# Opening of a hybrid decoder block: two quarters of x turned one unit sooner, two groups of sums moved with them

## The chip, the cores and the metric

The kernel runs on one core of a Trainium2 chip. The core has a matrix engine (TensorE, PE in the profile), three engines for elementwise work (VectorE or DVE, ScalarE or ACT, GpSimd or POOL), and SyncE (SP), which here issues nearly all loads. Each engine works through its own instructions in the order in which the program issues them; semaphores tie the engines together. The metric is the device time of one execution in microseconds (us); a kernel's time is the median of its runs.

## The reference

For one sequence of 256 rows and width 2048 the reference computes one decoder layer and a last normalisation, all in float32:

```
x = x + 0.5 * swiglu_ffn(rms_norm(x, ffn1_norm), gate, up, down)      # width 5632
z = rms_norm(x, mix_norm) @ w_in                                      # two head groups share z
y = concat(rms_norm(recurrent(z), ...), rms_norm(short_conv(z), ...))
x = x + y @ w_out
x = x + 0.5 * swiglu_ffn(rms_norm(x, ffn2_norm), gate, up, down)
out = rms_norm(x, final_norm)
swiglu_ffn(x, g, u, d) = (silu(x @ g) * (x @ u)) @ d
```

The change lies in the first some 50 us of the first feed-forward part: the first 512 columns of `x @ gate` and `x @ up`.

## The kernel before, in words

Every float32 matrix is multiplied in two parts. ACT copies it into a high part (`hi`, type fp32r), DVE subtracts that from the original and gives the low part (`lo`). A product is high by high, high by low and low by high, three matmuls of 128 x 128 by 128 x 512 each. For the stationary side x has to lie with its columns on the partitions, so x is turned: PE transposes 128 x 128 blocks into a PSUM bank, ACT scales the result by the norm's gain and writes the high part, DVE the low part. This is called a turn of a quarter of x (512 of the 2048 columns; tile `xT_n`). Eight transposes, four ACT copies and four DVE operations make one turn; `turn(c)` in `begin` (line 866) makes PE's part at once and returns two functions, `his` (ACT) and `los` (DVE).

The opening (`begin`, line 845) handles the first 512 columns of gate and up in eight units: quarter 0 to 3 of x with the gate block ("g") and with the up block ("u"). Its names: `fetch(u, m)` loads a unit's weights, `high` and `low` make its two parts on ACT and DVE, `mm` makes its 24 matmuls (16 with the high part of the weights, then 8 with the low part). `multiply` (line 436) has places at which a function can be called within a unit: `late` before the last eighth's low matmuls of the second half of the rows, `within` before the last four high matmuls when the unit is cut into pieces `js`. The order of instructions in `begin` is that of the text of the program, on every engine: nothing is rearranged.

Three weight rooms are used in turn, so a load waits on SP until the low part of the unit three loads earlier has been made; loads behind it on SP wait too.

After the opening the columns of gate and up are computed by a scheme with seven products instead of eight, of sums of quarters and sums of weights. The sums of x that it needs are made within the opening: `sums` (line 794) makes the first one, its high part on ACT and its low part on DVE (tile `xs`), and leaves five further steps to `more_sums(n)`: "two" (two additions), the parts of sum 5, the parts of sum 6, "last" (one addition), and the parts of sum 2. They need quarters 0 and 1 only. `fifth_sums` (line 812) makes the same for one block of 128 columns of quarters 2 and 3: six small DVE additions, a copy on ACT and a low part on DVE. `plain` makes the exact values of a quarter, `norm.squares` the sums of squares on ACT, and `norm.factor` the row factor, which needs all four quarters' squares (a few tiny DVE operations around a square root on ACT).

The order of the stage behind the opening (`fine_stage`, line 1406) is written by a planner that takes the engines' state at the end of the opening as constants (line 1583: `free = {"PE": 0.0, "DVE": -6.0, "ACT": -8.0, "SP": -14.0}`), so its order is the same before and after this change. Its first product ("p0") uses `raw_g_w` with `xT_n` into `ps_g_a`, its second ("p4") uses a sum of two weight blocks with `xs` into `ps_g_c`; then come the transposes `ph`, and a part with `raw_g_x` into `ps_g_e`. Between the low part of p0 and that of p4, DVE adds the weight blocks and multiplies the gated result of the opening (tile `sg`).

Of the kernel before, what the change touches and what calls it, by code (L numbers as in the profile page):

```python
# [176 lines left out]
def hybrid_block(ctx: ExitStack, tc: tile.TileContext, a: dict, out: bass.AP):  # L177
# [43 lines left out]
    def f32(ap):  # L221
        return ap.bitcast(F32)
# [82 lines left out]
    def big(name):  # L305

        return bigs.tile([P, UK, 2 * S], F32R, tag="big", name=name)
# [106 lines left out]
    def low_part(raw, hi, lo):  # L414
        dve.tensor_tensor(lo, raw, f32(hi), op=ALU.subtract)


    def blocks(hi, lo):
        return [(hi[:, j, :], lo[:, j, :]) for j in range(hi.shape[1])]
# [12 lines left out]
    def stationary(tile, t):  # L432

        return [(tile[:, j, t * P : (t + 1) * P], tile[:, j, S + t * P : S + (t + 1) * P]) for j in range(UK)]
# [212 lines left out]
    def quad(tile):  # L647
        return tile.rearrange("p (j c) -> p j c", j=UK)
# [107 lines left out]
    def ffn(tag, norm, after, opening=False):  # L756
        with tc.tile_pool(name=f"ffn{tag}", bufs=1, side="left", reuse_waits="tile") as fp:
            wg, wu, wd = (a[f"ffn{tag}_w_{s}"][0] for s in ("gate", "up", "down"))

            def keep(name, dt=F32):  # L760
                return fp.tile([P, CW], dt, tag="keep", name=name, bufs=11)
# [23 lines left out]
            def quads():  # L785
                if norm.exact is None:
                    return vs
                return {
                    (t, i): norm.exact[:, :, i * S + t * P : i * S + (t + 1) * P] for t in range(NT) for i in range(2)
                }  # L790
# [3 lines left out]
            def sums(meanwhile=None):  # L794
                pair = [big(f"xs{tag}_{i}") for i in range(2)]
                parts = [(b[:, :, o : o + P], b[:, :, o + P : o + S]) for b in pair for o in (0, S)]
                spare = quad(keep(f"spare{tag}"))
                two, last, high, low = seven_of(sf, units[halves[0]], units[halves[1]], quads(), spare, parts, meanwhile)

                def both(i):  # L800
                    high(i)
                    low(i)

                sum_of.extend([two, lambda: both(5), lambda: both(6), last, lambda: both(2)])

            def more_sums(n):
                for _ in range(n):
                    sum_of.pop(0)()
# [3 lines left out]
            def fifth_sums():  # L812
                v, w = keep(f"fifth{tag}"), keep(f"fifth_sums{tag}")
                for i, u in enumerate(plains):
                    x = f32(units[u])[:, 0]
                    dve.tensor_tensor(v[:, i * S : (i + 1) * S], x[:, :S], x[:, S:], op=ALU.add)
                (a11, a21), (a12, a22) = ([v[:, i * S + t * P : i * S + (t + 1) * P] for t in range(NT)] for i in range(2))
                s4, s5, s6, s2 = (w[:, i * P : (i + 1) * P] for i in range(4))
                dve.tensor_tensor(s4, a21, a22, op=ALU.subtract)
                dve.tensor_tensor(s6, a11, a21, op=ALU.subtract)  # L820
                dve.tensor_tensor(s5, s4, a11, op=ALU.subtract)
                dve.tensor_tensor(s2, a12, s5, op=ALU.add)
                home = units[halves[0]]
                high, low = (home[:, :, o + P : o + 2 * P] for o in (0, S))
                act.copy(high, quad(w))
                dve.tensor_tensor(low, quad(w), f32(high), op=ALU.subtract)
                fifth.update({i: (high[:, z, :], low[:, z, :]) for z, i in enumerate((4, 5, 6, 2))})
                one, two = ([stationary(units[u], t)[0] for t in range(NT)] for u in plains)
                fifth.update({0: one[0], 1: two[0], 3: two[1]})
# [8 lines left out]
            def first(u, m):  # L838
                return f"{m}{tag}_0_{u}", {"g": wg, "u": wu}[m][u * UK * P : (u + 1) * UK * P, :CW]
# [5 lines left out]
            def begin():  # L845

                raw, parts = {}, {}
                ends = ((0, 2), (2, UK))

                def fetch(u, m, pieces=((0, UK),), loaded=None):  # L850
                    n, src = first(u, m)
                    raw[u, m] = load(src, n, pieces, loaded)
                    parts[u, m] = split_tiles(n)

                def high(u, m, pieces=ends):
                    for i, e in pieces:
                        act.copy(parts[u, m][0][:, i:e, :], raw[u, m][:, i:e, :])

                def low(u, m, pieces=((0, UK),)):
                    for i, e in pieces:  # L860
                        low_part(*(z[:, i:e, :] for z in [raw[u, m]] + parts[u, m]))

                def mm(u, m, *more):
                    joint(u, m, blocks(*parts[u, m]), *more)

                def turn(c):
                    norm.xT[c] = big(f"xT_{norm.name}_{c}")
                    return norm.turn_in_steps(c, [xres[:, t, c * CW : (c + 1) * CW] for t in range(NT)], norm.xT[c])

                def products(j, which=slice(0, 2)):  # L870
                    hi, lo = blocks(*parts[0, "g"])[j]
                    for w, n in ((hi, 2), (lo, 1))[which]:
                        for t in range(NT):
                            for i, y in enumerate(stationary(norm.xT[0], t)[j][:n]):
                                pe.matmul(ps["g", t], y, w, start=(j, i) == (0, 0) and w is hi, stop=False, skip_group_check=True)

                quarters = tuple((j, j + 1) for j in range(UK))
                fetch(0, "g", quarters, lambda i: load_x(0, 2 * P) if i == 1 else None)
                for j in range(UK):
                    if j == 2:  # L880
                        products(1, slice(0, 1))
                    norm.turn((j,), True)
                    high(0, "g", quarters[j : j + 1])
                    low(0, "g", quarters[j : j + 1])
                    if j == 1:
                        keep_busy(1)
                        products(0)
                products(1, slice(1, 2))
                for j in range(2, UK):
                    products(j)  # L890

                fetch(0, "u", ends)
                load_x(1)
                fetch(1, "g", ends)
                load_x(2)
                load_x(3)
                js = (range(2), range(2, UK))
                high(0, "u", ends[:1])
                norm.squares(0, (0,))
                low(0, "u", ends[:1])  # L900
                high(0, "u", ends[1:])
                norm.squares(0, (1,))
                low(0, "u", ends[1:])
                plain(0)

                def second():
                    his, los = turn(1)
                    his()
                    los()

                norm.squares(1)
                mm(0, "u", None, None, js, second)

                high(1, "g")
                low(1, "g", ends)
                plain(1)
                norm.squares(2)
                mm(1, "g", None, None, js)

                fetch(1, "u")  # L920
                fetch(2, "g")
                norm.squares(3, (0,))
                high(1, "u", ends[:1])
                norm.squares(3, (1,))
                norm.factor()
                high(1, "u", ends[1:])
                low(1, "u", ends)
                high(2, "g")

                def third():  # L930
                    low(2, "g", ends[:1])
                    his, los = turn(2)
                    his()
                    los()

                mm(1, "u", None, third, js)
                low(2, "g", ends[1:])

                fetch(2, "u")
                high(2, "u")  # L940
                low(2, "u")
                fetch(3, "g")
                high(3, "g")
                sums()
                mm(2, "g")

                his, los = turn(3)
                his()
                los()
                low(3, "g")  # L950
                fetch(3, "u")
                high(3, "u")
                more_sums(1)
                low(3, "u")
                mm(2, "u")
                more_sums(4)
                fifth_sums()
                mm(3, "g")
                mm(3, "u")

# [1022 lines left out]
    with tc.tile_pool(name="outs", bufs=1, side="left", reuse_waits="tile") as op:  # L1983
# [10 lines left out]
        two, last_sum, high, low = seven_of(so, yT[0], yT[1], quads, spare, halves_of)  # L1994
# [148 lines left out]
    ends = {}  # L2143
# [56 lines left out]
```

## Time and profile before

| | |
|---|---|
| median of 3 runs | 1708.05 us (1707.28 to 1708.12) |
| profiled execution, its own time | 1707.82 us |
| its span, first to last instruction | 1706.0 us |
| PE busy | 1694.0 us (99%) |
| DVE busy | 1540.4 us (90%) |
| ACT busy | 1109.0 us (65%) |
| granted TensorE clock, mean | 0.999 |

PE is TensorE's matmuls, PEld its weight loads, which overlap the matmuls; an "q" behind an engine's name means its queue, where loads are issued. A row of the timeline has start, length, engine, line, operation, output and inputs, shapes, count, and in brackets how long the engine stood idle before and what ended the wait. Line 43 is a helper through which all instructions go, so tiles tell the groups apart. A group's length is that from its first start to its last end; instructions of one engine overlap a little at their ends. In a row of the view by stretches, the numbers are the stretch, its length, then for PE, PEld, DVE, ACT and POOL the busy time with the count, the granted clock, the share of the DMA engines and GB/s. A row of waits tells who waited for what, and total, times and longest in us.

### The profile page before, as it was taken

The page shows a single profiled execution, that of the slowest core. Times are in us where ns is not written, and L with a number is a line of the kernel's source. Part 1 is how long each engine was busy: PE and PEld are TensorE (multiplying, and loading weights), DVE is VectorE, ACT ScalarE, POOL GpSimd, SP SyncE. Part 2 cuts the span into 40 slices and gives each one's busy share as a digit, 9 for nine tenths or more (in the row PEclk, how much of TensorE's full clock was granted, in tenths as well). Part 3 has the DMA queues.
Part 4 walks back from the last instruction along what each step waited for, and adds up shares of the span by engine and source line. Part 5 has one row for each costly group of instructions (what it writes and reads, how often), then busy time and mean ns, then how long its engine had stood idle before and what let it go on. Part 6 is the DMA issues. An engine that isn't in the chain of part 4 may idle for free.

```text
span 1706.0 us, 20409 instructions
## 1 busy us (share of the span) xinstructions
PE 1694.0 (99%) x7869; PEld 1411.8 (83%) x7869; DVE 1540.4 (90%) x1330; ACT 1109.0 (65%) x1334; POOL 63.6 (4%) x96
## 2 busy tenths in 40 slices
PE   9999999999999999999999999999999999999998
PEld 7788888888888888888888888888888888888886
DVE  7999899999899999887897887998899998999997
ACT  6675566766666668567966665755666665667665
POOL 0200000000000000000000000000000000000000
PEclk9999999999999999999999999999999999999999
DMA  8777887768877868755565656767768878868784
GB/s 291 216 246 198 275 260 227 236 210 256 250 253 228 286 178 270 243 163 191 175 198 198 216 196 213 255 242 212 244 191 265 271 223 239 284 215 249 246 250 144
DMA packets 184432, 392.51 MB, mean 230 GB/s; under 512 B 7956, under 2 KB 10896, under 8 KB 178832
## 3 DMA queue, kind: packets, MB, share of 16 engines
q1 hardware_dynamic: 174912, 340.81, 57.5%
q0 software_dynamic: 9248, 49.36, 14.9%
q8 instruction: 61, 1.00, 0.2%
q10 hardware_dynamic: 176, 1.06, 0.1%
q14 instruction: 35, 0.29, 0.0%
HBM read 339.82 MB, written 2.10 MB: 200 GB/s over the span
## 4 chain that ended last, share of the span: by engine, by line
PE 98%; DVE 1%; issue 0%; ACT 0%; DVEq 0%
PE ps_in L43 10%; PE ps_u_a L43 10%; PE ps_g_a L43 10%; PE ps_d_a L43 9%; PE ps_u_c L43 6%; PE ps_g_c L43 5%; PE ps_d_c L43 5%; PE ps_u_d L43 4%; PE ps_g_d L43 4%; PE ps_d_d L43 4%; PE ps_d_e L43 4%; PE ps_d L43 4%; PE ps_g_e L43 3%; PE ps_o L43 3%; PE ps_u_e L43 2%; PE ps_g L43 2%
## 5 line engine op out<-in xcount | busy, mean ns | idle before, releaser
L43 ACT CAST hi_g_p<-raw_g_w 128x1024 fp32r<-128x1024 f32 (+1 forms) x140 | 172.6, 1263 | 116.2 <-DVE raw_g_w L43 43.6
L43 ACT CAST hi_u_p<-raw_u_w 128x1024 fp32r<-128x1024 f32 (+1 forms) x140 | 172.7, 1262 | 100.2 <-PE ps_u_a L43 41.6
L43 DVE TENSOR_TENSOR lo_g_p<-raw_g_w,hi_g_p 128x2560 fp32r<-128x2560 f32 (+2 forms) x90 | 199.3, 2227 | 31.9 <-ACT hi_g_p L43 11.5
L43 DVE TENSOR_TENSOR lo_u_p<-raw_u_w,hi_u_p 128x2560 fp32r<-128x2560 f32 (+2 forms) x90 | 199.5, 2228 | 14.4 <-ACT hi_u_p L43 11.6
L43 ACT CAST hi_d_p<-raw_d_w 128x1024 fp32r<-128x1024 f32 x140 | 141.2, 1047 | 79.8 <-DVE raw_d_w L43 39.6
L43 DVE TENSOR_TENSOR lo_d_p<-raw_d_w,hi_d_p 128x2048 fp32r<-128x2048 f32 (+1 forms) x90 | 162.4, 1813 | 11.7 <-ACT hi_d_p L43 10.3
L43 PE MATMUL ps_in<-xT_nm,hi_in 128*128 128x512 f32 x512 | 122.5, 391 | 0.0
L43 PEld LDWEIGHTS ps_in<-xT_nm,hi_in 128*128 128x128 f32 x512 | 94.0, 188 | 18.9 <-ACT tha L43 0.5
L43 ACT CAST hi_d_x<-raw_d_x 128x1024 fp32r<-128x1024 f32 x72 | 73.2, 1047 | 37.1 <-PE ps_d_c L43 11.9
L43 DVE TENSOR_TENSOR lo_in<-raw_in,hi_in 128x2048 fp32r<-128x2048 f32 x32 | 73.3, 2289 | 21.0 <-ACT hi_in L43 20.5
L43 DVE TENSOR_TENSOR lo_d_x<-raw_d_x,hi_d_x 128x2048 fp32r<-128x2048 f32 x36 | 82.1, 2286 | 7.1 <-ACT hi_d_x L43 7.1
L43 DVE TENSOR_TENSOR raw_u_w<-raw_u_w,raw_u_w 128x1024 f32<-128x1024 f32 (+2 forms) x50 | 86.7, 1755 | 0.7
L43 DVE TENSOR_TENSOR raw_g_w<-raw_g_w,raw_g_w 128x1024 f32<-128x1024 f32 (+2 forms) x50 | 86.4, 1754 | 0.8 <-DMA raw_g_w<-in_ffn_w_gate_dram 0.3
L43 ACT CAST hi_in<-raw_in 128x1024 fp32r<-128x1024 f32 x64 | 64.2, 1044 | 30.1 <-PE ps_in L43 16.3
L43 ACT CAST hi_g_x<-raw_g_x 128x1536 fp32r<-128x1536 f32 x40 | 59.2, 1480 | 19.4 <-DMA raw_g_x<-in_ffn_w_gate_dram 11.5
L43 DVE TENSOR_TENSOR lo_u_x<-raw_u_x,hi_u_x 128x1536 fp32r<-128x1536 f32 x40 | 70.1, 1751 | 0.3 <-issue 0.3
L43 DVE TENSOR_TENSOR lo_g_x<-raw_g_x,hi_g_x 128x1536 fp32r<-128x1536 f32 x40 | 70.0, 1751 | 0.0
L43 PEld LDWEIGHTS ps_in<-xT_nm,lo_in 128*128 128x128 f32 x512 | 65.6, 191 | 2.5
L43 ACT CAST hi_u_x<-raw_u_x 128x1536 fp32r<-128x1536 f32 x40 | 59.1, 1476 | 11.5 <-PE ps_u_c L43 5.7
L43 PE MATMUL ps_in<-xT_nm,lo_in 128*128 128x256 f32 x512 | 66.4, 283 | 0.0
L43 PE MATMUL ps_u_a<-hi_u_p,xT_n 128*128 128x512 f32 x240 | 61.1, 390 | 0.0
L43 PE MATMUL ps_g_a<-hi_g_p,xT_n 128*128 128x512 f32 x240 | 60.9, 389 | 0.0
(473 smaller groups left out, 3922.9 us busy)
## 6 DMA issues: line engine op xcount, KB each, us to landing
raw_g_w<-in_ffn_w_gate_dram SPq DMA_DIRECT2D x40, 1024.0 KB, 6.9
raw_u_w<-in_ffn_w_up_dram SPq DMA_DIRECT2D x40, 1024.0 KB, 6.0
raw_d_w<-in_ffn_w_down_dram SPq DMA_DIRECT2D x40, 1024.0 KB, 6.2
raw_d_x<-in_ffn_w_down_dram SPq DMA_DIRECT2D x36, 1024.0 KB, 6.2
raw_in<-in_w_in_dram SPq DMA_DIRECT2D x32, 1024.0 KB, 5.1
raw_g_x<-in_ffn_w_gate_dram SPq DMA_DIRECT2D x40, 768.0 KB, 7.7
raw_u_x<-in_ffn_w_up_dram SPq DMA_DIRECT2D x40, 768.0 KB, 7.1
raw_d_w<-raw_d_w POOLq DMA_DIRECT2D x20, 1024.0 KB, 7.4
```

What stands on the lines that cost most here:

```text
L43: ins = getattr(self.engine, name)(*args, **kwargs)
```

## The change

The third quarter of x is turned inside unit (1, g), before its last four high matmuls, where it was turned inside (1, u) before its last four low ones. The fourth quarter is turned inside (1, u) where it was turned behind (2, g). `sums` is called behind the low part of (1, u), before the parts of (2, g), where it was behind the parts of (2, u) and the high part of (3, g). Its further steps follow between the parts of the later units, and `fifth_sums` stands before the low part of (3, u), where it was behind everything. The low part of (2, g) is no longer split around a turn.

```diff
                 norm.squares(2)
-                mm(1, "g", None, None, js)
+
+                def turning(c):
+                    def fn():
+                        his, los = turn(c)
+                        his()
+                        los()
+
+                    return fn
+
+                mm(1, "g", None, None, js, turning(2))
 
                 fetch(1, "u")
                 fetch(2, "g")
...
                 low(1, "u", ends)
+                sums()
                 high(2, "g")
-
-                def third():
-                    low(2, "g", ends[:1])
-                    his, los = turn(2)
-                    his()
-                    los()
-
-                mm(1, "u", None, third, js)
-                low(2, "g", ends[1:])
+                low(2, "g", ends)
+                mm(1, "u", None, None, js, turning(3))
 
                 fetch(2, "u")
                 high(2, "u")
+                more_sums(1)
                 low(2, "u")
                 fetch(3, "g")
                 high(3, "g")
-                sums()
                 mm(2, "g")
 
-                his, los = turn(3)
-                his()
-                los()
+                more_sums(2)
                 low(3, "g")
+                more_sums(2)
                 fetch(3, "u")
                 high(3, "u")
-                more_sums(1)
+                fifth_sums()
                 low(3, "u")
                 mm(2, "u")
-                more_sums(4)
-                fifth_sums()
                 mm(3, "g")
                 mm(3, "u")
```

## The prediction

> **What bounds the kernel now.** First the page's head, then who waited for whom on TensorE over the whole span, then the same for its weight loads early on, then busy times by stretch.
>
> ```profile
> span 1706.0 us, 20409 instructions
> PE 1694.0 (99%) x7869; PEld 1411.8 (83%) x7869; DVE 1540.4 (90%) x1330; ACT 1109.0 (65%) x1334; POOL 63.6 (4%) x96
> ```
> ```profile
> PE ps_g_c L43 <- ACT hi_g_p L43: 1.8, 2, 1.0
> ...
> PE ps_g_c L43 <- DVE lo_g_p L43: 0.5, 1, 0.5
> ```
> ```profile
> PEld ps_g_e L43 <- DVE lo_g_x L43: 0.3, 1, 0.3
> ```
> ```profile
> 53.47:63.80 10.33, 7.96 (x32) 5.27 (x31) 10.29 (x8) 6.52 (x7) 4.39 (x6) 1.00 0.41 95
> 63.80:98.20 34.40, 34.40 (x156) 28.39 (x155) 33.91 (x21) 23.92 (x24) 5.22 (x11) 1.00 0.77 248
> ```
>
> PE is the bound: in the whole run it waits for data, apart from its very first instruction, only at ps_g_c. That is the second product right behind the opening. In the stretch 53.47 to 63.80 PE is busy 7.96 of 10.33 us while DVE is busy 10.29: there, and there alone, DVE sets the pace. From 63.80 on PE has no gap though DVE works 33.91 of 34.40, so what PE gains before 63.80 it keeps, if DVE gains as much. Now PE in order of time (start, length, count).
>
> ```profile
> 12.50 2.92 PE L43 MATMUL ps_u<-hi_u,xT_n 128*128 128x512 f32 x12
> 15.25 1.04 PE L43 MATMUL pt_n<-ident,xres 128*128 128x128 f32 x8
> ...
> 18.86 3.79 PE L43 MATMUL ps_g<-hi_g,xT_n 128*128 128x512 f32 x16
> ...
> 24.30 3.79 PE L43 MATMUL ps_u<-hi_u,xT_n 128*128 128x512 f32 x16
> ...
> 53.47 2.43 PE L43 MATMUL ps_g_a<-hi_g_p,xT_n 128*128 128x512 f32 x10
> 55.95 1.43 PE L43 MATMUL ps_g_a<-lo_g_p,xT_n 128*128 128x512 f32 x5
> 58.34 1.19 PE L43 MATMUL ps_g_c<-hi_g_p,xs 128*128 128x512 f32 x4 [0.97 <-ACT hi_g_p L43]
> 60.38 1.19 PE L43 MATMUL ps_g_c<-hi_g_p,xs 128*128 128x512 f32 x4 [0.85 <-ACT hi_g_p L43]
> ...
> 63.00 0.73 PE L43 MATMUL ps_g_c<-lo_g_p,xs 128*128 128x512 f32 x2 [0.50 <-DVE lo_g_p L43]
> ...
> 63.80 1.04 PE L43 MATMUL ph<-ident,sg 128*128 128x128 f32 x8
> ```
>
> A unit of 24 matmuls without a turn takes 24.30 - 18.86 = 5.44 us, 0.2267 each. A unit with a turn inside takes 18.86 - 12.50 = 6.36. The 30 matmuls of the first two products (53.47 to 63.80) would take 6.80; they take 10.33, so 3.53 us are lost there. That is what the change can win, with a few tenths of small losses beside it.
>
> **Why DVE is late: it idled before.** ACT first, then DVE.
>
> ```profile
> 15.89 1.57 ACT L43 ACTIVATE xT_n<-pt_n,cols_first 128x256 fp32r<-128x256 f32 x4 [0.98 <-PE pt_n L43]
> 17.33 2.01 ACT L43 CAST hi_g<-raw_g 128x1024 fp32r<-128x1024 f32 x2
> ...
> 20.75 0.64 ACT L43 ACTIVATE junk_n<-xres 128x512 f32<-128x512 f32 x1
> ...
> 21.38 1.03 ACT L43 CAST hi_u<-raw_u 128x1024 fp32r<-128x1024 f32 x1
> ...
> 23.58 1.03 ACT L43 CAST hi_u<-raw_u 128x1024 fp32r<-128x1024 f32 x1
> 24.51 1.99 ACT L43 CAST hi_g<-raw_g 128x1024 fp32r<-128x1024 f32 x2
> 29.48 1.57 ACT L43 ACTIVATE xT_n<-pt_n,cols_first 128x256 fp32r<-128x256 f32 x4 [2.97 <-PE pt_n L43]
> 30.92 2.01 ACT L43 CAST hi_u<-raw_u 128x1024 fp32r<-128x1024 f32 x2
> ...
> 50.62 2.42 ACT L43 CAST hi_g_p<-raw_g_w 128x1024 fp32r<-128x1024 f32 x2
> ...
> 60.23 1.47 ACT L43 CAST hi_g_x<-raw_g_x 128x1536 fp32r<-128x1536 f32 x1
> ```
> ```profile
> 24.37 2.36 DVE L43 TENSOR_TENSOR lo_u<-raw_u,hi_u 128x1024 fp32r<-128x1024 f32 x2
> ...
> 30.35 1.66 DVE L43 SCALAR_TENSOR_TENSOR xT_n<-pt_n,cols_first,xT_n 128x256 fp32r<-128x256 f32 x4 [2.49 <-ACT xT_n L43]
> ...
> 36.63 0.69 DVE L43 TENSOR_TENSOR xs<-spare,xs 128x512 fp32r<-128x512 f32 x1 [0.69 <-ACT xs L43]
> 37.75 1.66 DVE L43 SCALAR_TENSOR_TENSOR xT_n<-pt_n,cols_first,xT_n 128x256 fp32r<-128x256 f32 x4 [0.43 <-ACT xT_n L43]
> ...
> 47.64 0.69 DVE L43 TENSOR_TENSOR xs<-v,xs 128x512 fp32r<-128x512 f32 x1 [0.69 <-ACT xs L43]
> ...
> 50.74 0.69 DVE L43 TENSOR_TENSOR xT_n<-fifth_sums,xT_n 128x512 fp32r<-128x512 f32 x1 [0.69 <-ACT xT_n L43]
> 53.07 2.83 DVE L43 TENSOR_TENSOR lo_g_p<-raw_g_w,hi_g_p 128x2560 fp32r<-128x2560 f32 x1 [1.63 <-ACT hi_g_p L43]
> ...
> 65.67 1.75 DVE L43 TENSOR_TENSOR lo_g_x<-raw_g_x,hi_g_x 128x1536 fp32r<-128x1536 f32 x1
> ```
>
> From the low part of (1, u) at 24.37 to the first product's low part at 53.07 are 28.70 us, of which 2.49 + 0.69 + 0.43 + 0.69 + 0.69 + 1.63 = 6.62 idle: 22.08 of work. The 2.49 is the third quarter's turn (it waits for PE at 29 us), the 1.63 stands behind ACT, which could not begin hi_g_p at 50.62 before the fifth-slice copy.
>
> **The change, part by part.** No instruction is added or removed; eight transposes, four ACT and four DVE operations per turn, three sums groups and their copies change place. The order of loads stays.
>
> *Third quarter's turn inside (1, g).* PE reaches it at 18.86 + (15.25 - 12.50) = 21.61. ACT begins the copies 15.89 - 15.25 = 0.64 later, at 22.25, and is free 17.33 - 15.89 = 1.44 after that, at 23.69. Queued behind these copies on ACT are the fourth quarter's squares, both halves of hi_u of unit 1 and the norm's square root, so all move from 20.75 to 23.69, by 2.94. The fourth quarter's load is not late: its squares ran at 20.75 without a wait. The halves of hi_u end at 21.38 + 1.03 + 2.94 = 25.35 and 23.58 + 1.03 + 2.94 = 27.55. The low part of (1, u) follows the norm's factor on DVE and starts at 24.37 + 2.94 = 27.31.
>
> *PE's new waits.* (1, g) now takes 6.36 and ends at 25.22. (1, u) finds its first half at 25.35 + 0.05 (58.34 against the copy's end), 0.18 late; eight matmuls (1.81) later, at 27.21, it wants the second half, there at 27.60: 0.39. How much a restart costs no row gives alone: sixteen in step take 3.79, so four would take 1.07, and behind a wait they take 1.19, about 0.1. Bounds 0 and 0.2 each; I take 0.1 twice. Together 0.77. The fourth quarter's turn sits inside (1, u): 6.36 again. (1, u) ends at 25.22 + 6.36 + 0.77 = 32.35.
>
> *DVE from 27.31.* The third quarter's 1.66 now lie ahead of this point (in idle time before the factor), so 22.08 - 1.66 = 20.42 of work are left. Of the idle, three waits of 0.69 remain (a sum, its copy on ACT, its low part); the waits for turns and the 1.63 go; one is new: hi_g of unit 2 now stands behind the first sum's copy. That sum is ready at 27.31 + 2.3 + 0.68 = 30.29, its copy ends at 30.9, the half of hi_g (1.99 for two) at 31.9, and DVE, free at 31.66, waits 0.27. So the first product's low part starts at 27.31 + 20.42 + 2.34 = 50.1 instead of 53.07, 3.0 sooner. The sums cost nothing extra: they were on DVE before, and low (3, u), now last, ends at 50.1 where PE wants it 3.6 into that unit, about 52.3. ACT is through with the fifth-slice copy at 47 and with hi_g_p (2.42) at 49.5, before 50.1. If that cover of 0.6 went, its excess would come off the 3.0.
>
> *PE to the end of the stall.* PE wants hi_g of unit 2's second half at 33.26; it ends at 32.9: cover 0.3. Four units of 5.44 lead to 54.11, 0.64 later than now. Then 6.80 for the first two products without a wait, since DVE and the copies between are 3.0 sooner: 60.91 instead of 63.80, a gain of 2.89. The last low part of the second product, due at 60.23, comes 3.0 before 63.00, at 60.0: 0.2 to spare. The next tight place is lo_g_x, which already holds PE's weights for 0.3; on DVE it ends 3.0 sooner, so PE cannot gain more than about 3.0 in any case without DVE gaining more. Sum: 2.9 us.
>
> *Loads.* A load goes out when the low part that frees its room is done.
>
> ```profile
> 26.75 0.37 SPq L43 DMA_DIRECT2D raw_g<-in_ffn_w_gate_dram  x1
> ...
> 45.17 0.92 SPq L43 DMA_DIRECT2D raw_g_w<-in_ffn_w_gate_dram  x2
> 46.13 1.42 SPq L43 DMA_DIRECT2D raw_g_x<-in_ffn_w_gate_dram  x2
> ```
> ```profile
> raw_g<-in_ffn_w_gate_dram SPq DMA_DIRECT2D x1, 1024.0 KB, 5.3
> ```
> ```profile
> DMA to landing us min/median/max: 4.3/5.7/8.5
> ```
>
> The gate columns of unit 3 leave at 29.7 instead of 26.75 and land 5.3 later at 35.0; ACT comes to them about 36. Low (3, u) was done at 45.14 and ends at 50.1 now, so the fourth load of the next stage leaves at 50.2, raw_g_x behind it at 51.1 instead of 46.13. With at most 8.5 to landing it is there by 59.6, by the median 56.8. Its copy (1.47) ran at 60.23 and would now be free to run at 57.3; PE wants it at 60.91 + 0.79 = 61.7. So up to 59.6 + 1.5 = 61.1 it is covered, by 0.6.
>
> The page TensorE: Matmul & The Clock Gate of the Trainium skill (section Architectural detail) says that ACT and DVE are strict first-in first-out. It speaks against the change, as copies that wait for PE now hold the squares and hi_u. The trace agrees: hi_u at 30.92 ran only behind the copies that ACT had waited 2.97 us for. Were ACT free to pass them, the 0.77 would go and the sum be 3.7; by the rule it is 2.9.
>
> **Own time and median.** The profiled execution took 1707.82 us, span 1706.0 and 1.8 around it: 1704.9 after. The median of the runs is 1708.05, so the forecast is 1705.1. I take 0.2% (3.4 us) as what can be told from no change.
>
> **Rivals.**
> - *The whole loss goes.* If (1, u) finds hi_u in time (0.57 of waiting and 0.2 of restarts were overpriced) and DVE's waits shrink likewise, PE gains 3.53 plus the 0.3 at lo_g_x and some tenths: up to 4.2, so 1703.9. For it: half a microsecond decides. Against it: ACT's order is fixed, and the copies cannot start before PE's transposes.
> - *DVE starts later than I count.* Every 1 us by which low (1, u) starts after 27.31, or by which a copy behind ACT holds DVE, comes off the gain. With 2 us: 1707.1. For it: three links (transposes, copies, squares and factor) in a row, with PE waiting too. Against it: each link has its row.
> - *The load takes the stall's place, slower than before.* raw_g_x leaves 5.0 later and its user is 2.9 earlier. If it lands after 64.59 - 1.5 = 63.1 (64.59 is 63.80 + 0.79), 12 us after its issue, nothing is won; at 14 us PE loses 2: 1710. It decides from 61.7 - 1.5 = 60.2 on, 9.1 us after issue. Against it: the longest landing of this kind is 8.5, and the queue is only 0.41 full in 53.47 to 63.80.
> - *It does nothing.* If the stall were due to its own loads or to PE, 1708.0. Against it: the waits at 58.34 to 63.00 name ACT and DVE, and DVE is busy 10.29 of 10.33.
>
> **Chances.** The forecast 0.52, by itself 1704.4 to 1705.9; the whole loss 0.20; DVE late 0.18; the load 0.06; nothing 0.04. The range 1703.7 to 1707.6 leaves out the load, the far end of nothing and the edges, under 0.2. Faster by over 0.2% means under 1704.6: most of the second case and a slice of the first, 0.26. Slower by over 0.2% is the far part of the load, with what I have not thought of, 0.06. The rest, 0.68, is within 0.2%.
>
> **What would show it.** Copies of xT_n on ACT near 22.3 and squares at 23.7; PE waiting at ps_u of unit 1 for hi_u, twice, 0.2 and 0.4; lo_g_p at 50.1 on DVE with no idle ahead of it; PE through ps_g_c without a wait and ph at 60.9; raw_g_x issued near 51. I am wrong if PE still waits at ps_g_c, if raw_g_x appears as a releaser of ACT for more than 3 us, or if low (1, u) starts after 28.

## The result, and the profile after

The changed kernel takes 1704.88 us (median of 20 runs, 1704.42 to 1706.92), the kernel before 1707.74 (20 runs beside it, 1707.28 to 1708.32): 2.86 us less, a ratio of 0.9984 with a 95% interval of 0.9977 to 0.9990. The forecast was 1705.1, a gain of 2.9 us on the 1708.05 of the first three runs. The profiled execution took 1704.92 us with a span of 1703.0.

Who waited for whom on PE over the whole span of the changed kernel (total, times, longest in us):

```profile
span 1703.0 us, 20410 instructions
```
```profile
PE idle L43 <- DVE ones L43: 1.1, 1, 1.1
PE ps_in_c_a L43 <- DVE lo_in_c_p L43: 0.3, 1, 0.3
```

The waits at ps_g_c are gone. A wait of 0.3 us has appeared at ps_in_c_a, at 731.8 us; it is told of below. The stretch in which PE had been busy 7.96 of 10.33 us now reads (stretch, length, busy PE, PEld, DVE, ACT, POOL with counts, clock, DMA share, GB/s):

```profile
53.47:63.80 10.33, 10.33 (x51) 8.67 (x50) 10.33 (x9) 7.09 (x9) 7.35 (x10) 1.00 1.07 324
```

DVE is as full as before, but PE is full as well: DVE's work now lies 3 us ahead. PE in order of time, the rows that answer to those before:

```profile
12.66 2.91 PE L43 MATMUL ps_u<-hi_u,xT_n 128*128 128x512 f32 x12
...
19.02 2.88 PE L43 MATMUL ps_g<-hi_g,xT_n 128*128 128x512 f32 x12
21.74 1.03 PE L43 MATMUL pt_n<-ident,xres 128*128 128x128 f32 x8
...
23.54 1.99 PE L43 MATMUL ps_g<-lo_g,xT_n 128*128 128x512 f32 x8
25.55 3.38 PE L43 MATMUL ps_u<-hi_u,xT_n 128*128 128x512 f32 x12
...
32.39 3.79 PE L43 MATMUL ps_g<-hi_g,xT_n 128*128 128x512 f32 x16
...
54.15 2.43 PE L43 MATMUL ps_g_a<-hi_g_p,xT_n 128*128 128x512 f32 x10
56.41 1.30 PE L43 MATMUL ps_g_a<-lo_g_p,xT_n 128*128 128x512 f32 x5
57.55 1.98 PE L43 MATMUL ps_g_c<-hi_g_p,xs 128*128 128x512 f32 x8
...
60.95 1.03 PE L43 MATMUL ph<-ident,sg 128*128 128x128 f32 x8
```

The first unit here starts at 12.66 instead of 12.50, before anything that was changed, so 0.16 is to be taken from the times of the changed kernel when the two are compared. The price is seen at 25.55: (1, u) starts 0.2 late, and its twelve matmuls last 3.38 where those at 19.02 last 2.88, 0.5 for the second half of hi_u. (The 0.2 is 25.55 against 19.02 + 6.36 = 25.38, the time of a unit with a turn inside.) The gain is seen at 57.55: eight matmuls in one piece, where before they came in two fours with a wait each. From the first unit to ph are 60.95 - 12.66 = 48.29 us; before they were 63.80 - 12.50 = 51.30. That is 3.01 us.

ACT and DVE around the same places:

```profile
22.38 1.57 ACT L43 ACTIVATE xT_n<-pt_n,cols_first 128x256 fp32r<-128x256 f32 x4 [1.51 <-PE pt_n L43]
23.82 0.65 ACT L43 ACTIVATE junk_n<-xres 128x512 f32<-128x512 f32 x1
...
46.65 0.62 ACT L43 CAST xT_n<-fifth_sums 128x512 fp32r<-128x512 f32 x1 [0.59 <-DVE fifth_sums L43]
47.18 2.42 ACT L43 CAST hi_g_p<-raw_g_w 128x1024 fp32r<-128x1024 f32 x2
...
58.38 1.48 ACT L43 CAST hi_g_x<-raw_g_x 128x1536 fp32r<-128x1536 f32 x1 [1.00 <-DMA raw_g_x<-in_ffn_w_gate_dram]
```
```profile
27.45 2.35 DVE L43 TENSOR_TENSOR lo_u<-raw_u,hi_u 128x1024 fp32r<-128x1024 f32 x2
...
32.04 2.36 DVE L43 TENSOR_TENSOR lo_g<-raw_g,hi_g 128x1024 fp32r<-128x1024 f32 x2 [0.26 <-ACT hi_g L43]
...
47.91 2.29 DVE L43 TENSOR_TENSOR lo_u<-raw_u,hi_u 128x2048 fp32r<-128x2048 f32 x1
50.12 2.82 DVE L43 TENSOR_TENSOR lo_g_p<-raw_g_w,hi_g_p 128x2560 fp32r<-128x2560 f32 x1
```

hi_g_p on ACT begins at 47.18 instead of 50.62, and lo_g_p on DVE follows low (3, u) with no idle time at 50.12 instead of 53.07.

The 3 us stay. By plain difference of the times, the group ps_u_a<-hi_u_p, at 131.36 before, has a gain of 2.95 us, and ps_in at 704.33 and 708.07 still 2.95; around 760 it is 2.71, after the new wait at ps_in_c_a, and 2.91 in the last products. So PE carried the gain through without a stall that gave it back; the wait of 0.3 took a part of it for a while, and the last products have it again.

### The profile page after: what moved, and what is told of

It reads as the page before. It is cut to its first block, busy times and chain, and to the rows that moved or that the text cites. A ratio compares the mean times of both kernels' runs of the same rounds, so it can differ in the third digit from the quotient of the medians.

```text
span 1703.0 us, 20410 instructions
## 1 busy us (share of the span) xinstructions
PE 1693.2 (99%) x7869; PEld 1413.0 (83%) x7869; DVE 1540.2 (90%) x1330; ACT 1108.4 (65%) x1334; POOL 63.7 (4%) x96
## 4 chain that ended last, share of the span: by engine, by line
PE 57%; DVE 0%; issue 0%; DVEq 0%; ACT 0%
PE ps_in L43 9%; PE ps_u_a L43 5%; PE ps_g_a L43 5%; PE ps_d_a L43 5%; PE ps_u_c L43 3%; PE ps_g_c L43 3%; PE ps_o L43 3%; PE ps_d_c L43 3%; PE ps_u_d L43 2%; PE ps_g_d L43 2%; PE ps_d_d L43 2%; PE ps_d_e L43 2%; PE ps_d L43 2%; PE ps_g_e L43 2%; PE ps_u L43 1%; PE ps_o_q_x L43 1%
```

## The experiments

Each kernel was timed in five rounds beside the kernel before. The intervals of the ratios are about 0.0009 wide to either side, 1.5 us, so the times alone do not tell apart what differs by less; for that the text goes by the traces, one profiled execution of each kernel. For each run the table gives the stretch from the first matmul of (0, u) to ph, which leaves the start out.

| kernel | median, us (before beside it) | ratio, interval | (0, u) to ph, us | less than before |
|---|---|---|---|---|
| before | | | 51.30 | |
| the change | 1704.88 (1707.74) | 0.9984, 0.9977 to 0.9990 | 48.29 | 3.01 |
| turns only | 1707.00 (1707.82) | 0.9996, 0.9987 to 1.0005 | 50.05 | 1.25 |
| sums only | 1704.71 (1707.82) | 0.9982, 0.9973 to 0.9991 | 48.54 | 2.76 |
| fifth-slice sums last | 1707.81 (1707.82) | 1.0002, 0.9993 to 1.0011 | 51.19 | 0.11 |
| unit (1, u) first | 1703.97 (1707.82) | 0.9977, 0.9968 to 0.9986 | 47.63 | 3.67 |
| before, one line moved | 1706.86 (1707.89) | 0.9993, 0.9984 to 1.0002 | 50.32 | 0.98 |
| the change, work added | 1706.24 (1707.89) | 0.9988, 0.9979 to 0.9997 | 49.45 | 1.85 |
| unit (1, u) first, work added | 1704.10 (1707.89) | 0.9977, 0.9967 to 0.9988 | 47.59 | 3.71 |

**The turns alone.** Against the kernel before:

```diff
-                mm(1, "g", None, None, js)
+                mm(1, "g", None, None, js, turning(2))
...
-                mm(1, "u", None, third, js)
-                low(2, "g", ends[1:])
+                low(2, "g", ends)
+                mm(1, "u", None, None, js, turning(3))
...
                 mm(2, "g")
-
-                his, los = turn(3)
-                his()
-                los()
```

> The kernel before with the two turns moved and nothing else; sums and fifth-slice sums stay behind the units. Theory (DVE's idle time and the copy of the fifth-slice sums ahead of hi_g_p set the stall): the turns give back DVE's 2.49 us of waiting for PE, but start (1, u) 2.9 us later, and hi_g_p on ACT still stands behind the fifth-slice copy, so lo_g_p starts near 52.0 instead of 53.07 (50.1 with the whole change): 1.1 to 1.4 us faster than before, PE still waiting at ps_g_c for about 1.5. Rival (the sooner turns are what wins): 2.5 to 3 us faster, lo_g_p near 50.

Measured 0.8 us less by the medians, under the 1.1 expected and with an interval that holds no change, and 1.25 by the trace, as expected. PE's waits over the span are there again, halved:

```profile
PE ps_g_c L43 <- ACT hi_g_p L43: 0.7, 1, 0.7
PE ps_g_c L43 <- DVE lo_g_p L43: 0.5, 1, 0.5
```
```profile
49.49 0.69 DVE L43 TENSOR_TENSOR xT_n<-fifth_sums,xT_n 128x512 fp32r<-128x512 f32 x1 [0.69 <-ACT xT_n L43]
51.81 2.83 DVE L43 TENSOR_TENSOR lo_g_p<-raw_g_w,hi_g_p 128x2560 fp32r<-128x2560 f32 x1 [1.63 <-ACT hi_g_p L43]
```

DVE comes to lo_g_p at 51.81, 1.26 sooner, and the 1.63 us behind ACT are untouched. The turns by themselves bring less than half of the gain.

**The sums alone.** The turns stay; the kernel before with

```diff
                 low(1, "u", ends)
+                sums()
                 high(2, "g")
...
                 high(2, "u")
+                more_sums(1)
                 low(2, "u")
                 fetch(3, "g")
                 high(3, "g")
-                sums()
...
+                more_sums(2)
                 low(3, "g")
+                more_sums(2)
                 fetch(3, "u")
                 high(3, "u")
-                more_sums(1)
+                fifth_sums()
                 low(3, "u")
                 mm(2, "u")
-                more_sums(4)
-                fifth_sums()
```

> The kernel before with sums, their further steps and the fifth-slice sums moved as in the change, and both turns left in their old places. Theory: DVE has work to do while PE is not yet at the turns, and PE doesn't wait for hi_u of unit 1 (0.77 us less lost than in the whole change); lo_g_p starts near 50.0, ph near 60.5: 2.8 to 3.4 us faster than before, the same as the whole change or a few tenths better. Rival (the sooner turns are what wins): under 1.5 us faster.

Measured 3.1 us less by the medians, as the whole change within what the times can tell; 2.76 by the trace, 0.25 short of it, where as much or a few tenths more was expected. DVE's rows say why most of the gain is there:

```profile
30.37 1.66 DVE L43 SCALAR_TENSOR_TENSOR xT_n<-pt_n,cols_first,xT_n 128x256 fp32r<-128x256 f32 x4 [0.46 <-ACT xT_n L43]
...
37.80 1.66 DVE L43 SCALAR_TENSOR_TENSOR xT_n<-pt_n,cols_first,xT_n 128x256 fp32r<-128x256 f32 x4 [1.10 <-ACT xT_n L43]
...
50.06 2.82 DVE L43 TENSOR_TENSOR lo_g_p<-raw_g_w,hi_g_p 128x2560 fp32r<-128x2560 f32 x1
```

The wait of 2.49 us at the third turn has shrunk to 0.46, because the first sum runs in it; at the fourth turn DVE waits 1.10 (0.43 before). lo_g_p starts at 50.06, near the 50.12 of the whole change; counted from the first matmul of (0, u) (12.25 here) it is 0.35 later. PE does not wait for hi_u at (1, u) here, but it does wait for DVE in the second product, which the whole change does not:

```profile
59.99 0.73 PE L43 MATMUL ps_g_c<-lo_g_p,xs 128*128 128x512 f32 x2 [0.19 <-DVE lo_g_p L43]
```

So the sooner turns are not needed for most of the gain. They give DVE the last third of a microsecond, and PE pays for them at (1, u).

**The fifth-slice sums last again.** Against the changed kernel:

```diff
-                fifth_sums()
                 low(3, "u")
+                fifth_sums()
```

> The whole change, but fifth_sums behind low (3, u) again instead of ahead of it. Theory: the same DVE work in another order; but ACT's hi_g_p stands behind the fifth-slice copy, which now comes 2.2 us later, so lo_g_p starts near 53.1 on DVE after an idle time of 1.7 and the stall at ps_g_c is back: 0 to 0.6 us faster than before. The loads of the next stage leave 1.8 us sooner (low (3, u) ends near 48.3). Rival (the loads behind low (3, u) set the start of the next stage): faster than the whole change, by up to 1 us. Rival (only the amount of idle time on DVE in the opening counts): about as the whole change.

Measured: nothing is left of the gain (1707.81 against 1707.82; 0.11 us by the trace). In this kernel ACT, DVE and PE read:

```profile
49.87 0.62 ACT L43 CAST xT_n<-fifth_sums 128x512 fp32r<-128x512 f32 x1 [4.08 <-DVE fifth_sums L43]
50.40 2.42 ACT L43 CAST hi_g_p<-raw_g_w 128x1024 fp32r<-128x1024 f32 x2
```
```profile
45.82 2.29 DVE L43 TENSOR_TENSOR lo_u<-raw_u,hi_u 128x2048 fp32r<-128x2048 f32 x1 [1.20 <-ACT hi_u L43]
...
52.85 2.83 DVE L43 TENSOR_TENSOR lo_g_p<-raw_g_w,hi_g_p 128x2560 fp32r<-128x2560 f32 x1 [1.63 <-ACT hi_g_p L43]
```
```profile
58.13 1.20 PE L43 MATMUL ps_g_c<-hi_g_p,xs 128*128 128x512 f32 x4 [0.69 <-ACT hi_g_p L43]
60.17 1.20 PE L43 MATMUL ps_g_c<-hi_g_p,xs 128*128 128x512 f32 x4 [0.84 <-ACT hi_g_p L43]
```

Two waits took the gain, not one: 1.63 us behind ACT's copy, as expected, and 1.20 because low (3, u) now comes before ACT is through with hi_u. Together they are 2.83 of the 2.90 lost. The same amount of DVE work in another order is worth the whole gain. The loads of the next stage left about 2 us sooner here (raw_g_x issued from 49.10 on against 51.23) and nothing came of it; but here the waits for ACT and DVE hold that stage. That the loads do not hold it in the change is read from the change's own trace, where PE comes to raw_g_x's copy 1.9 us after it is done.

**Unit (1, u) ahead of the third turn.** Against the changed kernel:

```diff
                 norm.squares(2)
+                norm.squares(3)
+                fetch(1, "u")
+                fetch(2, "g")
+                norm.factor()
+                high(1, "u", ends)
+                low(1, "u", ends)
...
                 mm(1, "g", None, None, js, turning(2))
-
-                fetch(1, "u")
-                fetch(2, "g")
-                norm.squares(3, (0,))
-                high(1, "u", ends[:1])
-                norm.squares(3, (1,))
-                norm.factor()
-                high(1, "u", ends[1:])
-                low(1, "u", ends)
```

> The whole change, but squares of the fourth quarter, the norm's factor and both parts of (1, u) stand ahead of the third quarter's turn on ACT and DVE. Theory (ACT's order costs PE the two waits at (1, u) and puts low (1, u) on DVE 2.9 us later): no wait of PE at ps_u for hi_u, low (1, u) from about 24, lo_g_p near 48.1, ph near 60.0: 3.5 to 4.0 us faster than before, 0.7 to 1.0 better than the whole change. Rival (those waits overlap with something that binds anyway): as the whole change, 2.9.

Measured 3.85 us less by the medians, 3.67 by the trace, 0.66 better than the change by the trace: just under the 0.7 expected, and what the change paid at (1, u), 0.67. ACT has hi_u done before it comes to the copies of the turn, without idle time between, and PE goes through (1, u) in step:

```profile
22.56 1.98 ACT L43 CAST hi_u<-raw_u 128x1024 fp32r<-128x1024 f32 x2
24.45 1.56 ACT L43 ACTIVATE xT_n<-pt_n,cols_first 128x256 fp32r<-128x256 f32 x4
```
```profile
25.01 2.89 PE L43 MATMUL ps_u<-hi_u,xT_n 128*128 128x512 f32 x12
```

Twelve matmuls last 2.89 instead of 3.38, and begin with no gap. lo_g_p starts at 47.86 on DVE, ahead of need. This version is the fastest of all that ran, level with the same one with work added (below).

**One line moved in the kernel before.** Only this:

```diff
                 more_sums(1)
-                low(3, "u")
                 mm(2, "u")
                 more_sums(4)
                 fifth_sums()
+                low(3, "u")
```

> The kernel before with one line moved: low (3, u) on DVE stands behind the fifth-slice sums instead of ahead of (2, u)'s matmuls; turns and all sums stay. Theory: the fifth-slice copy on ACT comes 2.2 us sooner, hi_g_p behind it too, so the 1.63 us of idle time ahead of lo_g_p goes and lo_g_p starts near 51.6 to 52.2 instead of 53.07; PE now waits about 1 us for low (3, u) itself at ps_u, near 51.5. Net 0.8 to 1.5 us faster than before, about a third to a half of the change. Rival (only DVE's idle time at the turns counts): no change.

Measured 1.0 us less by the medians (the interval just holds no change), 0.98 by the trace. The 1.63 us behind ACT are gone, lo_g_p starts at 51.79, and a new wait of PE has come, as expected:

```profile
51.92 2.12 PE L43 MATMUL ps_u<-lo_u,xT_n 128*128 128x512 f32 x8 [0.45 <-DVE lo_u L43]
```

That wait is shorter than expected, 0.45 instead of about 1 us. A wait of DVE that was not expected says why no more than 1 us came of the 1.63:

```profile
43.29 1.29 DVE L43 TENSOR_TENSOR xs<-v,xs 128x512 fp32r<-128x512 f32 x2 [0.69 <-ACT xs L43]
```

In the kernel before, low (3, u) stood here and DVE had work while ACT made the copy of xs. 1.63 - 0.69 = 0.94, near the 0.98 measured. So the order of the fifth-slice sums against low (3, u) is worth about 1 us in the kernel before and all of the gain within the change, because an operation that is moved out of one wait uncovers another. The parts do not add up on their own: the turns alone and this one line have 1.25 + 0.98 = 2.23 of the 3.01.

**Work added.** Twice the same addition, once to the change and once to the version with unit (1, u) first; half of low (3, u) is computed a second time:

```diff
                 low(3, "u")
+                low(3, "u", ends[:1])
```

> The whole change, with the first half of low (3, u) computed a second time on DVE (1.16 us of work added, the same values). Theory: behind the opening DVE sets PE's pace with 0.1 to 0.3 us of cover, so 0.9 to 1.2 us of the gain go: 1.7 to 2.1 us faster than before, and PE waits at ps_g_c for lo_g_p again. Rival (the cover is larger and the 2.9 was set by PE's own order): as the whole change, 2.9.

> The version with unit (1, u) ahead of the third turn, with the same 1.16 us of DVE work added. Theory: there DVE is ahead of PE by about 1.3 to 1.5 us at lo_g_p and lo_g_x, so the added work is covered: 3.6 to 3.9 us faster than before, as without it, within 0.2. Rival (any DVE work in the opening costs its length): 1.1 us slower than without it, 2.7 faster than before.

The added work is 1.26 us on DVE: low (3, u) took 2.29 in the change, and the two together take 3.55:

```profile
47.94 3.55 DVE L43 TENSOR_TENSOR lo_u<-raw_u,hi_u 128x2048 fp32r<-128x2048 f32 x2
```

In the change it costs 1.2 by the medians against the kernel before (2.86 less became 1.65 less, just under the 1.7 expected) and 1.16 by the trace (3.01 became 1.85). PE waits for lo_g_p again:

```profile
61.32 0.73 PE L43 MATMUL ps_g_c<-lo_g_p,xs 128*128 128x512 f32 x2 [0.47 <-DVE lo_g_p L43]
```

In the version with unit (1, u) first the same work cost nothing that can be told (3.85 less became 3.79, and 3.67 became 3.71). There PE no longer waits for DVE in the first two products, and its weights for ps_g_e only 0.2 us:

```profile
PEld ps_g_e L43 <- DVE lo_g_x L43: 0.2, 1, 0.2
```

How far DVE is ahead of PE can be read at lo_g_x, the next thing that PE needs from it. In the change lo_g_x is done 0.11 us before PE's first matmul with it (64.45 against 64.56); in the version with unit (1, u) first 1.34 before (62.20 against 63.54), as expected; there with the work added 0.07 (63.62 against 63.69). So the added work took up the cover of 1.3 us and no more. In the change there was 0.1 to take: it moved PE and DVE forward by nearly the same 3 us and left them tight against each other.

## Why the prediction was right, step by step

- *What can be won.* The 3.53 us lost at ps_g_c are gone. 0.67 were paid at (1, u), and 0.13 because a turn inside a unit costs 6.36 - 5.44 = 0.92 where the fourth, behind (2, g), had cost 0.79. Small losses of 0.16 and 0.11 at (2, g) and (2, u) went too (sixteen matmuls in 3.95 and 3.90 before, 3.79 after). In sum 3.00; the stretch shows 3.01 where 2.89 was forecast.
- *The third turn on ACT and what stands behind it.* Forecast 22.25 for the copies and 23.69 for the squares; measured 22.38 and 23.82, less the 0.16 of the start 22.22 and 23.66. Low (1, u) was forecast for 27.31; measured 27.45, less 0.16 it is 27.29.
- *PE's waits at (1, u).* Forecast 0.18 and 0.39 with 0.1 twice for restarts, 0.77 in sum; measured 0.17 and 0.50, 0.67 in sum. That leaves 0.1 for the two restarts together, where 0.2 was taken; the bounds given, 0 and 0.2 each, hold it. This is most of the 0.12 by which the gain was forecast too small. That ACT's order causes these waits was argued only; the version with unit (1, u) first shows it.
- *DVE's sum.* From low (1, u) to lo_g_p 20.42 of work and 2.34 of idle time were forecast, 22.76; measured 50.12 - 27.45 = 22.67. The wait of 0.27 for hi_g is there as 0.26.
- *ACT's cover of 0.6 ahead of lo_g_p.* hi_g_p ends at 47.18 + 2.42 = 49.60, 0.5 before lo_g_p. That this cover carries much of the gain, which the prediction said only in passing, the run with the fifth-slice sums last shows: without it the wait of 1.63 is back.
- *DVE as the next bound.* The prediction allowed no more than about 3.0, as DVE itself would come only 3.0 sooner. The added work shows it: in the change 1.16 of its 1.26 us come through. PE's wait is then for lo_g_p at ps_g_c, where the prediction saw 0.2 to spare; at lo_g_x, which the prediction named as the next tight place, only PE's weights wait.
- *Loads.* raw_g_x was forecast to leave at 51.1 and land by 59.6; it left at 51.23 and ACT waited 1.0 us for it until 58.38. Its copy ended at 59.86, and PE wanted it at 61.74: covered by 1.9. The rival with the loads did not come.
- *The whole loss goes.* This rival did not come from the change (0.67 us of waits at (1, u) remain). With unit (1, u) first, which the prediction did not consider, the time is the rival's 1703.9 (1703.97), but the gain is 3.67 to 3.85 of its 4.2; the forecast counted from 1708.05, the kernel before beside that run took 1707.82.
- *What the prediction did not see.* In its own terms DVE gains 1.66 + 2.49 + 0.43 = 4.58 from the turns, less the 2.94 by which low (1, u) starts later: 1.64. The new wait for hi_g takes 0.27 of it, and the order at the end, fifth-slice sums ahead of low (3, u), gives 1.63. The turns alone brought 1.26 on DVE, with 0.5 lost to a longer wait for the copy of xs (1.19 instead of 0.69), so this share was about right. But it took the sums as moving along with nothing to gain. The run with the sums alone shows that the first sum fills 2.03 of the 2.49 that DVE waited at the third turn, so that 2.76 of the 3.01 are there with the turns in their old places.

## What to carry to other kernels

On engines that work in order, look in the timeline for the operations that wait for another engine, and ask what stands behind them that could go ahead of them; here the same instructions in another order were worth 2.9 us by the medians and 3.0 by the trace, and 3.9 and 3.7 in the best order that ran. Put work that waits for nothing (sums of what is there already) into the waits rather than behind them, and let whatever another engine's next stage needs first be done before the long operation, not after; but look first at which wait the long operation filled where it stood. When two engines are tight against each other, a gain on one is capped by the other: add a known amount of work to see how much cover there is.

## What the runs showed of the hardware that was not expected

The first 12 us differ between profiled executions though nothing in them was changed: the first matmul of (0, u) starts at 12.50 in the kernel before, 12.66 in the changed one, 12.25 with the sums alone, 12.19 with one line moved. The first four transposes of x, in the sums alone, in the kernel before and in the changed one:

```profile
4.13 0.66 PE L43 MATMUL pt_n<-ident,xres 128*128 128x128 f32 x4
```
```profile
4.13 1.02 PE L43 MATMUL pt_n<-ident,xres 128*128 128x128 f32 x4
```
```profile
4.13 1.11 PE L43 MATMUL pt_n<-ident,xres 128*128 128x128 f32 x4
```

They start at the same time in all three and take longer from one to the next. The first matmul with hi_g behind them takes 0.77 in the changed kernel and 0.47 in the kernel before. The record of the granted clock in each trace begins with the full clock, and it begins 3.94 us after the first instruction with one line moved, 4.10 with the sums alone, 4.92 in the kernel before and 6.59 in the changed one. (The views count the time ahead of that record as full clock.) Over the nine traces (0, u) starts later the later this record begins, but for three that lie within 0.02 us of each other. That goes with a slower TensorE clock in the first microseconds, for a time that differs from one execution to the next; what sets that time was not tried. The loads do not seem to hold the late ones: with the sums alone, one of the earliest, PE waits for a copy of the first weights,

```profile
PE ps_g L43 <- ACT hi_g L43: 0.3, 1, 0.3
```

and in the changed kernel it does not wait there. So for changes of a few tenths of a microsecond a stretch measured from behind this start tells more than the time of the whole.

The wait at ps_in_c_a (0.2 to 0.3 us), far behind the opening, is in the traces of the change, of the turns alone, of the fifth-slice sums last and of the change with work added, and not in those with the sums alone, with one line moved or with unit (1, u) first; what brings it about was not tried and stays open.
